# A hybrid conformer and dilated-attention trunk on one core: chunk 6 convolved with banded matrices that are loaded, a first stage in another order, and other rules for what GpSimd may take at a handover

## The chip, the cores and the metric

One core of one Trainium2 chip runs the whole kernel. The metric is device time in microseconds (us) of one execution, as the median of several runs.

## The reference

Two layers over 512 positions of width 1024. Layer 0 is a conformer convolution module and a gated feed-forward block (FFN); layer 1 is dilated attention with three branches and another FFN. Keys and values are projected once, after layer 0.

```python
def conformer_conv_module(h, w_in, b_in, dw, dw_b, ln_g, ln_b, w_out, b_out):
    u = h @ w_in + b_in
    u = u[..., :D_MODEL] * jax.nn.sigmoid(u[..., D_MODEL:])
    u = causal_dwconv(u, dw, dw_b)              # width 31, per channel
    u = layer_norm(u, ln_g, ln_b)               # over the 1024 channels
    u = jax.nn.silu(u)
    return u @ w_out + b_out

for i in range(DEPTH):                          # DEPTH = 2, N_A = 1
    h = rms_norm(x, mix_pre_g[i])
    y = conformer_conv_module(h, ...) if i < N_A else dilated_mixture_attention(h, ...)
    x = x + rms_norm(y, mix_post_g[i])
    x = x + rms_norm(conv_ffn(rms_norm(x, ffn_pre_g[i]), ...), ffn_post_g[i])
```

## The kernel before

Activations lie transposed: channels on the 128 partitions, 512 positions along the free axis, so that the 1024 channels are eight *chunks* (KC = 8). Every matrix product is made with three fp32r matmuls (`mm3`): weight and activation are each split into a high part (ScalarE: `whi`, `hh`, `uh`, `sh`) and a low part that is what the rounding left (VectorE: `wlo`, `hl`, `ul`, `sl`), and high x high, high x low and low x high are added up in PSUM. Weights come as 242 *units* of at most 128x1024 in the order in which TensorE uses them. `loader` issues their DMAs on SyncE's queue (SP) into two `raw` buffers; `splitter` makes the high part on ScalarE and the low part on VectorE or, where a line of its code finds GpSimd (Pool) early enough, on Pool. A ring holds 7 split units.

**The order of all five engines is written out by the builder.** Python generators (`spawn`) stand for side chains; each yields until a modelled clock (`Clock`) says that its engine and its operands are ready, and the instruction is put into the program there. `Clock.cost` holds the durations of that model; TensorE's were columns / 2400 + 0.0015 us for one pass. What is emitted is a fixed order per engine: a wrong guess of the model is a wait on the chip.

**The conformer stage** has these parts.
- *First loop* (`conformer`, L1060 on): for each of 8 input chunks the splits `hh` and `hl` and the square of x, which Pool makes for chunks 0 to 4 (`SQ_POOL`) and ScalarE for the others; VectorE adds the squares into `xacc` inside the same loop. TensorE takes the first two units as the splits come. `rchain` turns `xacc` into the scale `R` that every eviction of the stage needs.
- *Gate*: per chunk m two products (`cig`, `cia`) of 24 matmuls each; `gate` evicts them with R, a sigmoid and a product to `u`.
- *Depthwise convolution of 31 taps*, in three ways. Chunks in `CONV_PE` (1, 3, 5) go to TensorE as fp32 matmuls (`cv`) with banded matrices `T`, nine tiles per chunk that Pool builds out of a small table (`conv_taps`), 36 matmuls per chunk; their u goes through DRAM to another layout (`ud`, `ug`) and the result comes back the same way (`od`, `co`). Chunks 0, 2 and 4 are done tap by tap on VectorE, the last `POOL_TAPS` of them on ScalarE and Pool. Chunks in `MIXES` (6, 7) are split by halves of 256 positions: the first `MIX_PE` taps (17 and 20) on TensorE as three fp32r matmuls each with diagonal matrices (`cm`), the others on VectorE. Their input product is made by halves as well (`cim`). `MIX_PLAN` orders them: a and b are the input products of the first and second half, c and d the tap matmuls.
- *Layer norm*: `stat_acc` gathers sums of the chunks on Pool as they come and marks "stats"; `layer_norm` for each half adds the last chunk of `MIXES`, makes scale and shift and applies them (`ln`, `sh`, `sl`); `conv_out` is the product `wo`.

**A handover** is the change from one block's output to the next block's input: after the conformer (to the first FFN), after the first FFN (to keys and values, `kq`), after attention (to the second FFN). There `Junction.chain` (once for each half `hf`) makes two RMS norms out of sums on TensorE (`st`), a power on Pool (`rst`) and a broadcast (`bc`), and VectorE and ScalarE update x and split it. In `splitter`, `quiet` keeps the low splits of units near a handover off Pool: those from `QUIET[0]` before to `QUIET[1]` after the first unit of the next block; `chains` > 0 does the same, and is raised only inside `stat`.

Of the kernel before, what the change touches and what calls it, by code (L numbers as in the profile page):

```python
# [21 lines left out]
KC = 8  # L22
# [8 lines left out]
N_STAGED = 2  # L31
CONV_PE = (1, 3, 5)
MIXES = (6, 7)
MIX_PE = (17, 20)
MAIN_BANKS = 7
TURN = 8
SLACK = 0.3
POOL_BIAS = -1
QUIET = (3, 5)
SPILL_GAP = 2.5  # L40
# [6 lines left out]
P_CDVE = 3.5  # L47
POOL_TAPS = (8, 8, 4)
P_PTAPS = 3.5
# [135 lines left out]
class Clock:  # L185
# [28 lines left out]
    def cost(self, kind, name, out, ins):  # L214
        n = 1
        for d in out.shape[1:]:
            n *= d
        if name in ("tensor_reduce", "matmul", "transpose"):
            m = 1
            for d in ins[-1 if name == "matmul" else 0].shape[1:]:  # L220
                m *= d
            n = m
        if kind == "dve":
            fast = name in ("tensor_copy", "tensor_scalar") and len(ins) == 1 and ins[0].space == bass.MemoryType.SB
            scal = 0.065 if len(ins) > (2 if name == "scalar_tensor_tensor" else 1) and name[-6:] != "tensor" else 0.0
            scal = 0.065 if name == "scalar_tensor_tensor" and len(ins) > 2 else scal
            return 0.067 + scal + n / (1920.0 if fast else 960.0)
        if kind == "act":
            return (0.075 if name == "copy" else 0.188 if len(ins) > 1 else 0.094) + n / 1200.0
        if kind == "pool":  # L230
            if n <= 8:
                return 0.3 + 0.165 * n
            return 0.15 + n / 476.0
        passes = 4 if ins[0].dtype == F32 else 1
        if name == "transpose":
            return 0.107
        if passes == 1:
            return max(n, 256) / 2400.0 + 0.0015
        return 4 * max(n, 128) / 2400.0 + 0.0015

# [55 lines left out]
class Junction:  # L296
# [59 lines left out]
    def chain(self, hf, rest=None):  # L356
# [92 lines left out]
class Builder:  # L449
    def __init__(self, tc, ctx, x_d, w_d, vec_d, cvec_d, const_d, out_d):  # L450
# [4 lines left out]
        self.vec_d, self.const_d = vec_d, const_d  # L455
        nc = self.nc
# [206 lines left out]
    def splitter(self):  # L663

        nc, free = self.nc, self.clock.free
        for u in range(2, len(self.order)):
# [10 lines left out]
            at = self.clock.ready(hi[:, :w])  # L677
            if u not in self.quiet and not self.chains and max(free["pool"], at) + w / 476.0 + POOL_BIAS < max(free["dve"], at) + w / 960.0:
# [126 lines left out]
    def conv_taps(self, w_idx, Ts):  # L805

        nc = self.nc
        cv = self.c2("cv", F32, (128, 148))
        nc.sync.dma_start(cv, self.cvec_d[w_idx])
        T = []  # L810
        for q in range(ND):
            yield self.when("pool", cv)
            t = self.c2("T", F32, (128, 4, 32, 4))
            wv = cv[:, q * 16:q * 16 + 16].rearrange("p (d f) -> p d f", d=4)
            nc.gpsimd.tensor_tensor(t, self.chan[:, None, :, None].to_broadcast([128, 4, 32, 4]),
                                    wv[:, :, None, :].to_broadcast([128, 4, 32, 4]), op=ALU.mult)
            T.append(t)
        Ts[w_idx] = (T, cv)
        self.mark(("T", w_idx))

    def conv_pe(self, u_of, CO):
# [23 lines left out]
        def back(i, m, pc, cv):  # L845
            og = self.c2("og", F32, (128, 4, 128))
            yield self.when("act", pc)
            for g in range(4):
                nc.scalar.activation(og[:, g], pc[:, g * 128:(g + 1) * 128], AF.Identity,
                                     bias=cv[:, 144 + g:145 + g])  # L850
            self.done(pc)
# [9 lines left out]
        for i, m in enumerate(CONV_PE):  # L861
# [5 lines left out]
            for g in range(4):  # L867
                for d in range(ND):
                    nc.tensor.matmul(pc[:, g * 128 + d:(g + 1) * 128],
                                     T[(g * ND + d) // 4][:, (g * ND + d) % 4].rearrange("p c f -> p (c f)"),  # L870
                                     ug[:, g, :128 - d], start=d == 0, stop=d == ND - 1)
                    if d % 3 == 2:
                        yield W_CONV
# [185 lines left out]
    def conformer(self):  # L1059
# [5 lines left out]
        acc = self.c2("xacc")  # L1065
        sq = []

        def add(c):
            nc.vector.tensor_tensor(acc, sq[0] if c == 1 else acc, sq[c], op=ALU.add)

        for k in range(KC):
            g = self.v("mix_pre0", k)
            self.split_hi(Hc[k], full, self.X[k], g)
            self.split_lo(Hc[k], full, self.X[k], g)
            if k < len(PIECES):
                self.first_units(k)
            t = self.c2("sq")
            if k < SQ_POOL:
                nc.gpsimd.tensor_tensor(t, self.X[k], self.X[k], op=ALU.mult)
            else:  # L1080
                nc.scalar.activation(t, self.X[k], AF.Square)
            sq.append(t)
            if k > ADD_LAG:
                add(k - ADD_LAG)
        for c in range(KC - ADD_LAG, KC):
            add(c)
        self.next_unit = 2
# [723 lines left out]

def pack_cvec(inp):
    dw, dwb = inp["cm_dw"][0], inp["cm_dw_b"][0]
    out = np.zeros((len(CONV_PE), 32, 4, 148), np.float32)
    for i, m in enumerate(CONV_PE):
        for g in range(4):
            c = m * 128 + g * 32 + np.arange(32)
            for f in range(4):
                for d in range(ND):
                    for fo in range(4):  # L1820
                        s = 4 * d + fo - f
                        if 0 <= s <= 30:
                            out[i, :, f, g * 36 + d * 4 + fo] = dw[30 - s, c]
                out[i, :, f, 144 + g] = dwb[c]
    return out.reshape(len(CONV_PE), 128, 148)

# [23 lines left out]
```

## Time and profile before

| | |
|---|---|
| median of 3 runs | 1517.67 us (1514.81 to 1517.68) |
| the profiled execution | 1521.31 us, its span 1519.5 us |
| TensorE busy (matmul) | 1487.6 us, 98% |
| VectorE, ScalarE, GpSimd busy | 951.3, 603.8, 284.3 us |
| mean granted TensorE clock | 0.987 |

Matmuls are pipelined and their ends are modelled, so TensorE counts as busy in nearly all stretches; what a stage loses is seen only when the count of its matmuls, times the distance from start to start of two of them, is set against its length. The conformer stage lies at 0 to 224 us of the span, the first FFN from 224, keys, queries, values and attention from 597 to 1076, the output product and the second FFN after that.

### The profile page before, as it was taken

The page shows a single profiled execution, that of the slowest core. Times are in us where ns is not written, and L with a number is a line of the kernel's source. Part 1 is how long each engine was busy: PE and PEld are TensorE (multiplying, and loading weights), DVE is VectorE, ACT ScalarE, POOL GpSimd, SP SyncE. Part 2 cuts the span into 40 slices and gives each one's busy share as a digit, 9 for nine tenths or more (in the row PEclk, how much of TensorE's full clock was granted, in tenths as well). Part 3 has the DMA queues.
Part 4 walks back from the last instruction along what each step waited for, and adds up shares of the span by engine and source line. Part 5 has one row for each costly group of instructions (what it writes and reads, how often), then busy time and mean ns, then how long its engine had stood idle before and what let it go on. Part 6 is the DMA issues. An engine that isn't in the chain of part 4 may idle for free.

```text
span 1519.5 us, 19622 instructions
## 1 busy us (share of the span) xinstructions
PE 1487.6 (98%) x7778; PEld 1282.5 (84%) x7778; DVE 951.3 (63%) x1428; ACT 603.8 (40%) x1020; POOL 284.3 (19%) x169
## 2 busy tenths in 40 slices
PE   8999999999999999899999999999999999999997
PEld 6889998888888889789888889888898888888887
DVE  6997858946754758822556621566568846754745
ACT  5475465443432426423323222322355444432423
POOL 5894102301210200100000000100002301210212
PEclk9999999999999999999999999999999999999999
DMA  5430322333232222432222223222222332332311
GB/s 178 152 116 29 98 70 84 101 122 97 91 101 85 97 70 70 136 128 84 82 71 69 71 97 97 69 70 84 97 70 84 111 118 91 97 97 90 102 45 56
DMA packets 46891, 139.77 MB, mean 92 GB/s; under 512 B 5072, under 2 KB 10960, under 8 KB 46800
## 3 DMA queue, kind: packets, MB, share of 16 engines
q1 hardware_dynamic: 42768, 135.38, 27.9%
q10 hardware_dynamic: 4032, 3.15, 0.7%
q8 instruction: 61, 1.00, 0.3%
q14 instruction: 30, 0.25, 0.1%
HBM read 132.74 MB, written 5.77 MB: 91 GB/s over the span
## 4 chain that ended last, share of the span: by engine, by line
PE 86%; DVE 3%; ACT 1%; issue 1%; POOL 1%; DMA 0%; POOLq 0%; DVEq 0%; ACTq 0%
PE fi L171 31%; PE kq L171 17%; PE fo L171 16%; PE v L171 9%; PE wo L171 6%; PE sc L171 2%; PE pw L171 1%; PE cm L171 1%; PE pt L171 1%; PE pv L171 1%; PE cim L171 1%; DVE xacc L171 0%; DVE hl L171 0%; DVE mc L171 0%; PE st L171 0%
## 5 line engine op out<-in xcount | busy, mean ns | idle before, releaser
L171 ACT CAST whi<-raw 128x1024 fp32r<-128x1024 f32 (+2 forms) x242 | 248.3, 1027 | 545.7 <-PE fi L171 162.3
L171 POOL TENSOR_TENSOR wlo<-raw,whi 128x1024 fp32r<-128x1024 f32 (+1 forms) x71 | 172.1, 2425 | 929.3 <-ACT whi L171 929.1
L171 DVE TENSOR_TENSOR wlo<-raw,whi 128x1024 fp32r<-128x1024 f32 (+2 forms) x171 | 211.8, 1239 | 167.6 <-ACT whi L171 166.7
L171 PE MATMUL fi<-hl,whi 128*128 128x512 f32 (+1 forms) x768 | 289.3, 377 | 1.1 <-DVE hl L171 1.1
L171 PE MATMUL fi<-hh,whi 128*128 128x512 f32 (+1 forms) x768 | 290.2, 378 | 0.0
L171 PE MATMUL fi<-hh,wlo 128*128 128x512 f32 (+1 forms) x768 | 289.1, 376 | 0.0
L171 PEld LDWEIGHTS fi<-hl,whi 128*128 128x128 f32 x768 | 145.2, 189 | 29.2 <-DVE hl L171 1.3
L171 PEld LDWEIGHTS fi<-hh,whi 128*128 128x128 f32 x768 | 145.3, 189 | 28.2
L171 PEld LDWEIGHTS fi<-hh,wlo 128*128 128x128 f32 x768 | 145.2, 189 | 28.1
L171 PE MATMUL kq<-hh,whi 128*128 128x512 f32 (+1 forms) x416 | 165.0, 397 | 0.0
L171 PE MATMUL kq<-hl,whi 128*128 128x512 f32 (+1 forms) x416 | 157.6, 379 | 5.0 <-DVE hl L171 5.0
L171 PE MATMUL kq<-hh,wlo 128*128 128x512 f32 (+1 forms) x416 | 157.7, 379 | 0.7 <-DVE wlo L171 0.7
L171 PE MATMUL fo<-uh,whi 128*128 128x512 f32 (+1 forms) x416 | 150.1, 361 | 0.0
L171 PE MATMUL fo<-uh,wlo 128*128 128x512 f32 (+1 forms) x416 | 149.8, 360 | 0.0
L171 PE MATMUL fo<-ul,whi 128*128 128x512 f32 (+1 forms) x416 | 149.7, 360 | 0.0
L171 DVE SCALAR_TENSOR_TENSOR cc<-z,vec,cc 128x511 f32<-128x511 f32 (+1 forms) x176 | 142.6, 832 | 8.2 <-ACT cc L171 5.5
L171 DVE TENSOR_TENSOR z<-fi,R 128x512 f32<-128x512 f32 x88 | 60.1, 689 | 92.9 <-PE fi L171 89.2
L171 PEld LDWEIGHTS kq<-hl,whi 128*128 128x128 f32 x416 | 79.2, 190 | 17.3 <-DVE hl L171 5.4
L171 PEld LDWEIGHTS kq<-hh,wlo 128*128 128x128 f32 x416 | 78.7, 189 | 16.5 <-DVE wlo L171 0.9
L171 DVE TENSOR_TENSOR kq<-kq,R 128x512 f32<-128x512 f32 x48 | 46.0, 966 | 71.2 <-PE kq L171 70.5
L171 PEld LDWEIGHTS fo<-uh,whi 128*128 128x128 f32 x416 | 78.4, 188 | 12.8
L171 PEld LDWEIGHTS kq<-hh,whi 128*128 128x128 f32 x416 | 79.1, 190 | 11.9
(210 smaller groups left out, 2594.1 us busy)
## 6 DMA issues: line engine op xcount, KB each, us to landing
raw<-in_w_dram SPq DMA_DIRECT2D x222, 512.0 KB, 3.5
raw<-in_w_dram SPq DMA_DIRECT2D x18, 384.0 KB, 3.1
x<-in_x_dram SPq DMA_DIRECT2D x16, 256.0 KB, 4.3
xs<-x SPq DMA_DIRECT2D x8, 256.0 KB, 4.5
x<-xs SPq DMA_DIRECT2D x8, 256.0 KB, 5.7
out_dram<-x SPq DMA_DIRECT2D x16, 128.0 KB, 1.8
ud<-u ACTq DMA_DIRECT2D x3, 256.0 KB, 2.0
ug<-ud ACTq DMA_DIRECT2D x3, 256.0 KB, 2.7
```

The lines of the kernel that those rows point to most:

```text
L171: return f(*a, **k)
```

## The change

It does seven things. (1) Chunk 6 moves from `MIXES` to `CONV_PE`; chunk 7 alone is mixed, with 15 taps on TensorE in place of 20, and its order is a7 b7 c7 d7. (2) The matrices T are packed on the host and loaded: nine DMAs of 256 KB per chunk on SP's queue, two chunks ahead (`T_AHEAD`). (3) Chunk 4 gives 8 taps to ScalarE and Pool in place of 4. (4) In the first stage all squares are made on ScalarE and added on VectorE by side chains of low rank (`P_SQ`) after the splits. (5) The low splits of units under 6 stay on VectorE (`POOL_FROM`). (6) `QUIET` ends 1 unit after a handover's start in place of 5, but `chains` is raised from the first `chain` of a junction (not the last junction) to its end. (7) The model's TensorE durations are other ones.

```diff
-CONV_PE = (1, 3, 5)
-MIXES = (6, 7)
-MIX_PE = (17, 20)
+CONV_PE = (1, 3, 5, 6)
+MIXES = (7,)
+MIX_PE = (15,)
-QUIET = (3, 5)
+QUIET = (3, 1)
-POOL_TAPS = (8, 8, 4)
+POOL_TAPS = (8, 8, 8)
-SQ_POOL = 5
-ADD_LAG = 2
+P_SQ = 3
+POOL_FROM = 6
-MIX_PLAN = 'a6 a7 c6 c7 b6 b7 d6 d7'
+MIX_PLAN = 'a7 b7 c7 d7'
-T_AHEAD = 3
+T_AHEAD = 2
@@ Clock.cost
-        passes = 4 if ins[0].dtype == F32 else 1
         if name == "transpose":
-            return 0.107
-        if passes == 1:
-            return max(n, 256) / 2400.0 + 0.0015
-        return 4 * max(n, 128) / 2400.0 + 0.0015
+            return 0.111
+        if ins[0].dtype == F32:
+            return 4 * max(n, 128) / 2300.0
+        return max(n, 256) / 2286.0 + 0.0065
@@ Junction.chain
+        if hf == 0 and not self.last:
+            b.chains += 1
...
         b.mark((self, hf, "R"))
+        if hf == 1 and not self.kv:
+            b.chains -= 1
...
             yield from b.stat(self.rm, self.xacc, [slice(q, 512, 4) for q in range(4)])
+            b.chains -= 1
@@ splitter
-            if u not in self.quiet and not self.chains and ...
+            if u >= POOL_FROM and u not in self.quiet and not self.chains and ...
@@ conv_taps
-        cv = self.c2("cv", F32, (128, 148))
-        nc.sync.dma_start(cv, self.cvec_d[w_idx])
+        cv = self.small("cvb", [128, 4])
         for q in range(ND):
-            yield self.when("pool", cv)
-            t = self.c2("T", F32, (128, 4, 32, 4))
-            wv = cv[:, q * 16:q * 16 + 16].rearrange("p (d f) -> p d f", d=4)
-            nc.gpsimd.tensor_tensor(t, self.chan[...], wv[...], op=ALU.mult)
+            yield self.when("sp")
+            t = self.c2("T", F32, (128, 4, 128))
+            nc.sync.dma_start(t.rearrange("p d c -> p (d c)"), self.band_d[w_idx, :, q * 512:(q + 1) * 512])
             T.append(t)
+        nc.sync.dma_start(cv, self.cvec_d[w_idx])
@@ conformer
-            t = self.c2("sq")
-            if k < SQ_POOL:
-                nc.gpsimd.tensor_tensor(t, self.X[k], self.X[k], op=ALU.mult)
-            else:
+        def squares():
+            for k in range(KC):
+                yield self.when("act", self.X[k])
+                if k == 0:
+                    nc.scalar.activation(acc, self.X[k], AF.Square)
+                    continue
+                t = self.c2("sq")
                 nc.scalar.activation(t, self.X[k], AF.Square)
-            sq.append(t)
-            if k > ADD_LAG:
-                add(k - ADD_LAG)
+                self.spawn(add(k, t), P_SQ)
...
+        self.spawn(squares(), P_SQ)
         self.next_unit = 2
         self.spawn(self.loader(), 0)
...
         def rchain():
+            yield from self.until("xacc0")
```

## Rows read from the trace of the kernel before

**Rows 1.** The page's first part: busy time, share and count of each engine.
```profile
PE 1487.6 (98%) x7778; PEld 1282.5 (84%) x7778; DVE 951.3 (63%) x1428; ACT 603.8 (40%) x1020; POOL 284.3 (19%) x169
```

**Rows 2.** Stretches: length; PE, PEld, DVE, ACT, POOL busy (count); granted clock; DMA share, GB/s.
```profile
5.10:27.30 22.20, 17.79 (x48) 12.24 (x49) 19.16 (x19) 11.22 (x16) 10.47 (x6) 0.85 0.72 256
27.30:102.90 75.60, 73.77 (x398) 62.37 (x397) 70.52 (x90) 40.31 (x69) 67.41 (x49) 1.00 0.40 125
102.90:171.20 68.30, 65.98 (x521) 65.47 (x520) 56.81 (x116) 42.16 (x109) 28.05 (x20) 0.93 0.24 74
171.20:224.00 52.80, 50.76 (x412) 50.35 (x411) 33.02 (x74) 26.67 (x54) 3.99 (x4) 0.97 0.24 71
224.00:251.20 27.20, 26.10 (x216) 25.46 (x215) 22.91 (x54) 12.60 (x30) 6.30 (x4) 1.00 0.14 48
...
587.40:631.10 43.70, 37.39 (x303) 36.67 (x302) 40.93 (x94) 26.54 (x60) 8.76 (x7) 0.97 0.18 55
631.10:1076.60 445.50, 445.50 (x2185) 388.58 (x2186) 214.21 (x355) 135.31 (x242) 21.55 (x9) 1.00 0.28 89
...
1120.00:1160.00 40.00, 38.03 (x308) 37.53 (x308) 33.32 (x76) 21.03 (x50) 6.39 (x5) 0.96 0.23 69
```

**Rows 3.** The chain that ended last: start us, length us, what.
```profile
157.94 13.23 PE cm L171 x111
...
251.08 55.08 PE fi L171 x237
```

**Rows 4.** Timeline of TensorE: start us, length us, engine, operation, tiles, form, count.
```profile
84.36 0.82 PE L171 MATMUL cv<-ug,T 128*128 128x125 f32 x6
...
85.73 0.82 PE L171 MATMUL cv<-ug,T 128*128 128x122 f32 x6
```

**Rows 5.** Timeline of all engines in the first stage; the bracket: idle before, releaser.
```profile
16.66 5.19 POOL L171 TENSOR_TENSOR wlo<-raw,whi 128x1024 fp32r<-128x1024 f32 x2 [2.30 <-ACT whi L171]
16.70 2.92 DVE L171 SCALAR_TENSOR_TENSOR hl<-x,vec,hh 128x512 fp32r<-128x512 f32 x1
...
19.54 2.87 DVE L171 TENSOR_TENSOR xacc<-xacc,sq 128x512 f32<-128x512 f32 x1
...
23.12 0.50 PE L171 MATMUL cig<-hl,whi 128*128 128x512 f32 x1 [1.80 <-DVE hl L171]
...
23.59 0.74 DVE L171 SCALAR_TENSOR_TENSOR hl<-x,vec,hh 128x512 fp32r<-128x512 f32 x1
```

**Rows 6.** Waits of TensorE: who waited for whom, us in total, times, longest.
```profile
PE kq L171 <- DVE hl L171: 5.0, 1, 5.0
...
PE cv L171 <- DVE ca L171: 1.8, 1, 1.8
...
PE st L171 <- POOL m L171: 1.6, 1, 1.6
```

**Rows 7.** Timelines of ScalarE's queue, TensorE and Pool: chunk 5's way through the convolution.
```profile
108.53 0.34 ACTq L171 DMA_DIRECT2D ud<-u  x1
...
118.26 0.83 PE L171 MATMUL cv<-ug,T 128*128 128x128 f32 x6
...
133.17 0.38 ACTq L171 DMA_DIRECT2D od<-og  x1
...
142.76 1.48 POOL L171 TENSOR_TENSOR s<-s,sq 128x512 f32<-128x512 f32 x1
```

**Rows 8.** The chain that ended last, around the second half's layer norm.
```profile
180.27 0.79 PE lst L171 x8
...
187.25 27.55 PE wo L171 x215
```

**Rows 9.** Timelines of Pool and VectorE in the second handover.
```profile
616.20 2.47 POOL L171 TENSOR_TENSOR wlo<-raw,whi 128x1024 fp32r<-128x1024 f32 x1 [8.07 <-ACT whi L171]
616.34 2.61 DVE L171 SCALAR_TENSOR_TENSOR hl<-x,vec,hh 128x256 fp32r<-128x256 f32 x1
```

**Rows 10.** Stretches of 5 us (columns as in rows 2).
```profile
5.00:10.00 5.00, 4.50 (x9) 2.75 (x10) 2.97 (x5) 2.58 (x5) 1.14 (x2) 1.00 0.96 355
```

More of the change, by code (lines that the diff above doesn't have):

```diff
@@ L449, with __init__ @@
 class Builder:
-    def __init__(self, tc, ctx, x_d, w_d, vec_d, cvec_d, const_d, out_d):
+    def __init__(self, tc, ctx, x_d, w_d, vec_d, cvec_d, band_d, const_d, out_d):
         self.now = 0.0
@@ L454, in __init__ @@
         self.x_d, self.w_d, self.cvec_d, self.out_d = x_d, w_d, cvec_d, out_d
-        self.vec_d, self.const_d = vec_d, const_d
+        self.vec_d, self.band_d, self.const_d = vec_d, band_d, const_d
         nc = self.nc
@@ L677, in splitter @@
             at = self.clock.ready(hi[:, :w])
-            if u not in self.quiet and not self.chains and max(free["pool"], at) + w / 476.0 + POOL_BIAS < max(free["dve"], at) + w / 960.0:
+            if u >= POOL_FROM and u not in self.quiet and not self.chains and max(free["pool"], at) + w / 476.0 + POOL_BIAS < max(free["dve"], at) + w / 960.0:
                 eng = nc.gpsimd
@@ L807, in conv_taps @@
         nc = self.nc
-        cv = self.c2("cv", F32, (128, 148))
-        nc.sync.dma_start(cv, self.cvec_d[w_idx])
+        cv = self.small("cvb", [128, 4])
         T = []
         for q in range(ND):
-            yield self.when("pool", cv)
-            t = self.c2("T", F32, (128, 4, 32, 4))
-            wv = cv[:, q * 16:q * 16 + 16].rearrange("p (d f) -> p d f", d=4)
-            nc.gpsimd.tensor_tensor(t, self.chan[:, None, :, None].to_broadcast([128, 4, 32, 4]),
-                                    wv[:, :, None, :].to_broadcast([128, 4, 32, 4]), op=ALU.mult)
+            yield self.when("sp")
+            t = self.c2("T", F32, (128, 4, 128))
+            nc.sync.dma_start(t.rearrange("p d c -> p (d c)"), self.band_d[w_idx, :, q * 512:(q + 1) * 512])
             T.append(t)
+        nc.sync.dma_start(cv, self.cvec_d[w_idx])
         Ts[w_idx] = (T, cv)
@@ L849, in back @@
                 nc.scalar.activation(og[:, g], pc[:, g * 128:(g + 1) * 128], AF.Identity,
-                                     bias=cv[:, 144 + g:145 + g])
+                                     bias=cv[:, g:g + 1])
             self.done(pc)
@@ L869, in conv_pe @@
                     nc.tensor.matmul(pc[:, g * 128 + d:(g + 1) * 128],
-                                     T[(g * ND + d) // 4][:, (g * ND + d) % 4].rearrange("p c f -> p (c f)"),
+                                     T[(g * ND + d) // 4][:, (g * ND + d) % 4],
                                      ug[:, g, :128 - d], start=d == 0, stop=d == ND - 1)
@@ L1065, in conformer @@
         acc = self.c2("xacc")
-        sq = []
-        def add(c):
-            nc.vector.tensor_tensor(acc, sq[0] if c == 1 else acc, sq[c], op=ALU.add)
         for k in range(KC):
@@ L1076, in conformer, with add @@
                 self.first_units(k)
-            t = self.c2("sq")
-            if k < SQ_POOL:
-                nc.gpsimd.tensor_tensor(t, self.X[k], self.X[k], op=ALU.mult)
-            else:
-                nc.scalar.activation(t, self.X[k], AF.Square)
-            sq.append(t)
-            if k > ADD_LAG:
-                add(k - ADD_LAG)
-        for c in range(KC - ADD_LAG, KC):
-            add(c)
+        def squares():
[5 more added lines that the diff above has]
+                t = self.c2("sq")
+                nc.scalar.activation(t, self.X[k], AF.Square)
+                self.spawn(add(k, t), P_SQ)
+        def add(k, t):
+            while added[0] < k - 1:
+                yield 0.05
+            yield self.when("dve", t, acc)
+            nc.vector.tensor_tensor(acc, acc, t, op=ALU.add)
+            added[0] += 1
+            if added[0] == KC - 1:
+                self.mark("xacc0")
+        added = [0]
+        self.spawn(squares(), P_SQ)
         self.next_unit = 2
@@ L1809, in pack_vec, with pack_band @@
     return np.ascontiguousarray(np.concatenate([src[n].reshape(-1, 128).T for n, _ in VECS], 1))
[L1812 to L1815, printed above, removed]
+def pack_band(inp):
+    dw = inp["cm_dw"][0]
+    out = np.zeros((len(CONV_PE), 32, 4, 4, ND, 32, 4), np.float32)
+    i = np.arange(32)
+    for j, m in enumerate(CONV_PE):
         for g in range(4):
-            c = m * 128 + g * 32 + np.arange(32)
             for f in range(4):
@@ L1822, in pack_cvec @@
                         if 0 <= s <= 30:
-                            out[i, :, f, g * 36 + d * 4 + fo] = dw[30 - s, c]
-                out[i, :, f, 144 + g] = dwb[c]
-    return out.reshape(len(CONV_PE), 128, 148)
+                            out[j, i, f, g, d, i, fo] = dw[30 - s, m * 128 + g * 32 + i]
+    return out.reshape(len(CONV_PE), 128, 4 * ND * 128)
+def pack_cvec(inp):
+    dwb = inp["cm_dw_b"][0]
+    out = np.zeros((len(CONV_PE), 32, 4, 4), np.float32)
+    for j, m in enumerate(CONV_PE):
+        for g in range(4):
+            out[j, :, :, g] = dwb[m * 128 + g * 32:m * 128 + g * 32 + 32, None]
+    return out.reshape(len(CONV_PE), 128, 4)
 def kernel(**inputs):
@@ L1834 @@
         "cvec": pack_cvec(inp),
+        "band": pack_band(inp),
         "const": host_consts(),
```

## The prediction

> **What bounds the kernel now.** I read the page's engine shares first: TensorE is busy for 98% of the span [rows 1], so only its own work and the places where it stands or runs slowly can move the end. The busy share hides those places, because the ends of matmuls are modelled. So I took the distance from start to start: 237 matmuls of 512 columns in 55.08 us are 0.232 us each, and 111 of 256 columns in 13.23 us are 0.119 us each [rows 3]. Then I cut the span into stages and set count times distance against each length [rows 2]. The reader is to see that the stretch from 631 to 1077 us is busy without a break, while the time is lost in few places. The first two units need 48 x 0.232 = 11.2 us and take 22.2: 11.0 lost, of which 0.15 x 22.2 = 3.3 to the granted clock of 0.85 (part of the time at 1.2 GHz in place of 2.4). From 102.9 to 171.2 us stand 192 `cim` and 222 `cm` at 0.119 and one chunk of `cv` (8.1, below): 57.4 of 68.3, so 10.9 go to short sums, waits and a clock of 0.93. The `wo` stretch has 384 x 0.119 = 45.8 of 52.8. The three handovers hold 216, 303 and 308 matmuls at 0.119, which is 25.7 of 27.2, 36.1 of 43.7 and 36.7 of 40.0: 1.5, 7.6 and 3.3 lost. Last I read who ended TensorE's waits [rows 6].
>
> **Chunk 6 and the taps of chunk 7: TensorE's own work.** Chunk 6 loses 17 taps x 2 halves x 3 = 102 matmuls of 0.119, chunk 7 loses 5 x 2 x 3 = 30: -15.7 us. Added are 36 fp32 matmuls. Two groups of three `cv` start 1.37 us apart with three 512-column matmuls between [rows 4], so a group costs 1.37 - 0.70 = 0.67 us and a chunk 12 x 0.67 = 8.1. Chunk 6's input product changes from 96 x 0.119 = 11.4 to 48 x 0.232 = 11.2. Sum: **-7.9 us**, all on the path, the surest term (-7 to -8.5).
>
> **First stage.** VectorE's last `hl` starts at 23.59, and TensorE waits for one at 23.12 [rows 5]. Before it in VectorE's queue stand four additions into `xacc`, one held to 2.87 us, and an `hl` held to 2.92 where the clean one takes 0.74; both lie beside squares or low splits on Pool [rows 5]. Without them the last `hl` leaves 2.9 + 2.2 + 3 x 0.7 = 7.2 us earlier. TensorE then becomes the limit: 36 matmuls of chunks 2 to 7 are 8.4 us at the full clock. The start, until the first weights are there, stays. I take **-6 us** of the 11.0 lost; if half-clock stretches remain as long as now, -3; at most -8. The squares go to ScalarE behind the splits, their seven additions behind the `hl`, the low splits of units 2 to 5 to VectorE. All this is covered by TensorE's first two products and delays only R, which no one needs before the third pair of PSUM banks is full, some 33 us (three products of 11.2) after the start. Without that cover each added microsecond would count once.
>
> **The middle.** One `cv` group waits 1.8 us for a bank that VectorE's tap chain holds, one `st` 1.6 us for Pool's sums [rows 6]. 27 builds of T leave Pool, which is busy for 67 of 75.6 us [rows 2], and VectorE loses chunk 6's 13 taps x 2 and four taps of chunk 4. I take **-1.8** (0 to -4).
>
> **The loads of T.** 36 DMAs of 256 KB are 9.4 MB. The weights' stretch moves 125 GB/s over 75.6 us [rows 2], and the same queue has reached 355 GB/s [rows 10]. With T it would be 250 GB/s. SP's queue is passed by nothing else than weight loads; each waits there for a free `raw` buffer. The cover is the ring: six units ahead at 24 x 0.232 = 5.6 us are 33 us. Cost 0; what it costs uncovered is the third rival. T's own buffers fall from 27 to 18 in flight.
>
> **Layer norm, the step that I trust least.** Before, the first half's norm ran behind the second half's products. After, it needs chunk 6, which is the last to come and makes two trips through DRAM. Chunk 5's trip gives the legs [rows 7]: its product ends at 102.9 [rows 2], `cv` begins 15.4 us later, `og` leaves 14.9 us after that, Pool's last sum ends 11.1 us after `og`. From the last sums on TensorE to the first `wo` are 7.0 us [rows 8]. Let E6 be the end of chunk 6's product. Chunk 5's `cv` begins 15.4 - 11.2 = 4.2 us after E6 and takes about 12.5 when mixed with other matmuls, so chunk 6's begins at E6 + 16.7; with 14.9 + 11.1 + 7.0 the product `wo` can start at E6 + 49.7. TensorE's work after E6 is 11.4 for a7 and b7, 16.2 for two chunks of `cv`, 90 x 0.119 = 10.7 for c7 and d7 and about 1.5 of short sums: 39.8. So it stands some **10 us** in a place where it did not, and I add what the clock costs behind such a stop, 0.03 x 52.8 = 1.6 us in the `wo` stretch with its one stop [rows 2]: `wo` at E6 + 51.3 (45 if each leg is as short as it can be without Pool's holds, 58 if each adds 1 to 3 us). Against that, the second half's stop goes, because c7 and d7 are done by then: the `wo` stretch becomes about 49 in place of 52.8. E6 itself is 102.9 - 6 - 1.8 + 11.2 = 106.3. The stage ends at 106.3 + 51.3 + 49 = 206.6, not 224.0: **-17.4 us** in all, so the norm and its surroundings bring -1.7 beside the three terms above (-9 to +7).
>
> **Handovers.** Pool's low split from 616.20 holds an `hl` of VectorE to 2.61 us, until Pool has ended [rows 9]; the same happens four times in the three handovers (once, twice, once), and the long wait of `kq` for `hl`, 5.0 us [rows 6], lies behind two of them. After, the chain's whole length is closed to Pool. VectorE gets the four splits itself, about 1.3 us each (an estimate: twice the columns of the 0.74 row less its fixed part), in place of a hold of 2.1: net -0.9 x 4, and of the half-clock time behind the stops, 0.03 x 43.7 + 0.04 x 40 = 2.9 us, about half: **-5 us**. What VectorE does more is covered only where TensorE has staged matmuls; if TensorE waits for each added split instead, it is +5. Low end -9. After the chain, units 1 to 4 behind the start may now go to Pool, which the old `QUIET` forbade: that is in the +3 that I keep as the upper end.
>
> **TensorE's durations in the model.** The old model has 512 columns at 0.215 us, the trace 0.232. Short matmuls (`sc`, `pt`, `st`, `bc`) are therefore placed 8% late in the program, and no wait is seen from 631 to 1077 us. With the right figure they stand just where the model has their operands ready, and a Pool hold of 2 us can reach them. Pool has 9 instructions in that stretch [rows 2]: nothing or, at the worst, 9 x 2.1 = 19 us. The value lies nearest to the row that shows no wait: **+1**, and 4 as far as the range goes. Elsewhere the better order may gain as much.
>
> **Sum.** -17.4 - 5 + 1 = -21.4 us on 1521.3 us of the profiled execution (span 1519.5 and 1.8 around it), so 1499.9. That execution lies 3.6 us above the median of the runs, 1517.7; I shift by that: **1496.3 us**.
>
> **Rivals.** *The late chunk is later.* Every leg of chunk 6's trip grows and `wo` starts at E6 + 58 to 62, because its gate queues behind VectorE's taps: +7 to +11, some 1505. For it: chunk 5's gate needed 5.6 us before `ud` left. Against: 26 tap instructions less on VectorE. Chance 0.15. *The handovers do not get quieter*: VectorE, busy for 40.9 of 43.7 us in the second [rows 2], becomes the bound with added splits: +5 for -5, and with waits in attention +4, some 1508. Chance 0.13. *The loads of T stand before the weights*, the one that ends slower: if a T load waits on SP's queue for its buffer, the weights behind it wait too, and once more than the ring's 33 us are used up TensorE stops. At most all of T goes by while it stands: 9.4 MB at 355 GB/s are 26.6 us, so 1496 + 27 = 1523. Against: 18 buffers in place of 27, and two thirds of the bandwidth free [rows 2]. Chance 0.06. The Trainium skill, "DMA: Bandwidth & Descriptors", section "Queues, rings and completion order", says that each DMA engine takes one queue's descriptors in ring order, which is what would make this so; no run here shows T and weights on one queue yet. *The change does not do what it says* (T late, Pool still inside the chains): only TensorE's work falls, 1510. Chance 0.05.
>
> **How the numbers follow.** The forecast has the remaining 0.61. The terms' good ends together (-8.5, -8, -4, -9, -9, 0) would give 1479, which I hold for unlikely at once; half of that distance is 1487. Upwards the first two rivals and the last belong inside, so 1511. About 0.2% (3 us) is what a measurement of this kernel can tell from no change: faster than 1514.6 holds the forecast, the first two rivals and most of the last, 0.89; within, 0.05; slower than 1520.7, the loads' rival, 0.06.
>
> **What would show it.** Right: the first two units end near 21.5 us of the span; 90 `cm` in place of 222; `wo` starts near 158 us and ends near 207, after a stop of about 10 us; no `wlo` on Pool between the first `rst` and the last of a handover, and no VectorE row above 2 us there; the stretch of attention still without waits. Wrong: a wait of TensorE or ScalarE for `raw` between 30 and 100 us (the loads), or waits for `T`; a stop before `wo` of 20 us or more; `sc`, `pt` or `px` in the list of TensorE's waits.

## The result, and the profile after

The changed kernel takes **1497.5 us** (median of four runs, 1497.0 to 1498.1), against 1516.8 (1514.8 to 1517.7) for the kernel before beside it: a ratio of 0.9875, 95% interval 0.9858 to 0.9892. The forecast was 1496.3 us, in a range of 1487 to 1511. The time is right to 0.1%, but by luck: the gain comes from a cause that no step named, and the edits that the steps priced at -21 us are together worth about nothing, although some of the terms hold. What follows shows both.

The profiled execution took 1498.06 us, its span 1496.3. First line of its page, as in [rows 1]:

```profile
PE 1454.2 (97%) x7670; PEld 1265.6 (85%) x7670; DVE 907.8 (61%) x1431; ACT 593.8 (40%) x983; POOL 159.3 (11%) x106
```

TensorE's busy time fell by 33.4 us for 108 records fewer, although 72 of the new ones belong to 36 long fp32 matmuls, which leave two records each. 7.9 of that was expected. So I took the distance from start to start once more, in a stretch that the change does not touch, the first feed-forward. The chain that ended last, after, between 260 and 480 us (start us, length us, what):

```profile
336.35 87.04 PE fi L171 x384
423.39 43.52 PE fo L171 x192
```

and the same view of the kernel before:

```profile
339.61 89.24 PE fi L171 x384
```

The same 384 matmuls of 512 columns take 0.2267 us each and not 0.2324, as [rows 3] also has it. Both kernels run this stretch without a break at the full granted clock. A kernel has some 4,800 matmuls of this width: at 5 to 6 ns each that is 24 to 29 us, more than the whole gain. Matmuls of 256 columns come at medians of 0.118 to 0.122 us before and 0.120 after. ScalarE's rows are as before; VectorE's differ where Pool holds fewer of them (below).

Stretches of after, the first four cut at the same events as in [rows 2], the last one in the second handover (length; PE, PEld, DVE, ACT, POOL busy with counts; granted clock; DMA share, GB/s):

```profile
5.10:20.10 15.00, 12.75 (x48) 9.26 (x49) 12.41 (x18) 12.54 (x20) 0.00 (x0) 1.00 0.82 291
20.10:125.50 105.40, 91.35 (x469) 77.82 (x468) 83.83 (x110) 54.38 (x98) 51.80 (x35) 0.92 0.60 203
125.50:172.00 46.50, 43.97 (x348) 43.19 (x348) 32.20 (x67) 12.77 (x27) 12.54 (x9) 0.92 0.34 111
172.00:221.70 49.70, 48.31 (x405) 48.10 (x404) 32.30 (x80) 33.14 (x68) 1.50 (x2) 1.00 0.18 54
...
588.50:622.00 33.50, 28.01 (x222) 27.38 (x221) 31.60 (x73) 20.89 (x45) 3.71 (x4) 0.93 0.30 97
```

The first stage is 7.2 us shorter. The second row holds one chunk of products more (48 x 0.227 = 10.9 us) but is 29.8 us longer, and its clock fell from 1.00 to 0.92. The conformer ends at 221.7 us instead of 224.0; the forecast had 206.6. The second handover is still the place where VectorE is busy nearly all the time (31.6 of 33.5 us). Who ended TensorE's waits, after (us in total, times, longest), beside [rows 6]:

```profile
PE cv L171 <- DMA ug<-ud: 7.8, 2, 7.6
PE cv L171 <- issue: 6.0, 1, 6.0
PE kq L171 <- DVE hl L171: 4.4, 1, 4.4
PE py L171 <- DVE fr L171: 2.9, 2, 1.5
```

The first two rows are not in [rows 6] under these names, and both lie in the stretch where T is loaded. The third is the old wait of the second handover, hardly shorter. The fourth is new, in attention.

**The first new stop.** Timeline of after, TensorE and the DMA queues of SP and ScalarE (start us, length us, engine, line, operation, tiles, count; in brackets the idle time before and its releaser):

```profile
66.97 9.09 SPq L171 DMA_DIRECT2D T<-in_band_dram  x8
67.56 0.38 ACTq L171 DMA_DIRECT2D ug<-ud  x1
75.38 0.98 PE L171 MATMUL cv<-ug,T 128*128 128x128 f32 x3 [7.58 <-DMA ug<-ud]
```

and stretches of 5 us around it (columns as above):

```profile
65.00:70.00 5.00, 2.80 (x19) 2.20 (x17) 4.96 (x8) 4.16 (x10) 2.67 (x3) 1.00 0.65 203
70.00:75.00 5.00, 0.00 (x0) 0.00 (x0) 5.00 (x8) 0.70 (x1) 3.36 (x3) 0.62 1.01 322
75.00:80.00 5.00, 4.62 (x17) 4.27 (x18) 5.00 (x9) 2.11 (x3) 0.99 (x1) 0.50 0.82 256
```

Of the nine loads of T of this chunk six go out within 3.5 us on SP's queue (the other three from 75.3 on), and the shuffled chunk `ug`, 256 KB that TensorE needs at that moment, starts 0.6 us behind the first of them on ScalarE's queue. It lands after 7.7 us; in the kernel before the same transfer of the same chunk took 4.2. The DMA engines are full (1.01), and the clock is at half (1.2 GHz) for the 5 us behind TensorE's idle time. How long the transfers took between 5 and 130 us (KB each, median us from issue to landing), after:

```profile
T<-in_band_dram SPq DMA_DIRECT2D x36, 256.0 KB, 5.9
ug<-ud ACTq DMA_DIRECT2D x3, 256.0 KB, 3.5
od<-og ACTq DMA_DIRECT2D x2, 256.0 KB, 7.4
```

and before:

```profile
ug<-ud ACTq DMA_DIRECT2D x3, 256.0 KB, 2.7
od<-og ACTq DMA_DIRECT2D x2, 256.0 KB, 3.2
```

**The second new stop** has the same root at one remove. ScalarE's timeline of after:

```profile
95.32 0.40 ACTq L171 DMA_DIRECT2D od<-og  x1
...
103.29 0.37 ACTq L171 DMA_DIRECT2D co<-od  x1
103.75 0.59 ACT L171 COPY nm<-bc 128x512 f32<-128x512 f32 x1 [4.91 <-DMA od<-og]
...
116.75 0.34 ACTq L171 DMA_DIRECT2D ud<-u  x1
```

The way back of the second loaded chunk meets the next group of T loads and takes 8.0 us. ScalarE, which issues the load of `co` in its own queue, stands for 4.9 us; taps, diagonals, weight casts and the gate of the third loaded chunk queue up behind, and `ud` of that chunk leaves at 116.75. TensorE runs out of products at 115.7 and stands 6.0 us ("issue" in the list of waits), until that chunk's `ug` lands at 121.6.

### The profile page after: what moved, and what is told of

The parts are those of the page before. It is cut to its first block, busy times and chain, and to the rows that moved or that the text cites. A ratio compares the mean times of both kernels' runs of the same rounds, so it can differ in the third digit from the quotient of the medians.

```text
span 1496.3 us, 19325 instructions
## 1 busy us (share of the span) xinstructions
PE 1454.2 (97%) x7670; PEld 1265.6 (85%) x7670; DVE 907.8 (61%) x1431; ACT 593.8 (40%) x983; POOL 159.3 (11%) x106
## 4 chain that ended last, share of the span: by engine, by line
PE 89%; DVE 6%; DMA 2%; ACT 1%; issue 1%; POOL 0%; SPq 0%; ACTq 0%; POOLq 0%; DVEq 0%
PE fi L171 32%; PE kq L171 17%; PE fo L171 16%; PE v L171 9%; PE wo L171 6%; PE sc L171 2%; PE cv L171 2%; PE cia L171 1%; DVE mc L171 1%; DMA raw<-in_w_dram 1%; PE pw L171 1%; PE pt L171 1%; PE pv L171 1%; DMA T<-in_band_dram 1%; DVE wlo L171 1%
## 5 line engine op out<-in xcount | busy, mean ns | idle before, releaser
L171 DVE TENSOR_TENSOR wlo<-raw,whi 128x1024 fp32r<-128x1024 f32 (+1 forms) x204 | 251.6, 1234 | 166.8 <-ACT whi L171 166.6
L171 PE MATMUL fi<-hh,whi 128*128 128x512 f32 (+1 forms) x768 | 286.3, 373 | 0.0
L171 PE MATMUL fi<-hh,wlo 128*128 128x512 f32 (+1 forms) x768 | 285.4, 372 | 0.8 <-DVE wlo L171 0.8
L171 PE MATMUL fi<-hl,whi 128*128 128x512 f32 (+1 forms) x768 | 285.3, 371 | 0.0
L171 POOL TENSOR_TENSOR wlo<-raw,whi 128x1024 fp32r<-128x1024 f32 (+1 forms) x38 | 84.8, 2233 | 1010.3 <-ACT whi L171 1007.2
L171 PEld LDWEIGHTS fo<-ul,whi 128*128 128x128 f32 x416 | 78.6, 189 | 11.3
```

The costliest lines, as they stand in the source:

```text
L171: return f(*a, **k)
```

## The experiments

Ratios are to runs of the kernel before on the same chip, with 95% intervals.

**Is it the address?** The change adds four small tiles for the biases. Each takes 32 bytes per partition in the pool of small tiles, so all tiles of the main pool (`hh`, `hl`, `u`, `x`, `y`, T and the others) start 128 bytes later than before, while the weights `whi` and `wlo` stay where they were. This is read from the addresses of the compiled programs: modulo 256 bytes the weights lie at 192 in both kernels, the main pool at 64 before and at 192 after. The kernel before with nothing but this shift:

```diff
+        for _ in range(4):
+            nc.vector.memset(self.small("pad", [128, 4]), 0.0)
```

> The kernel before with one thing added: four unused tiles of 4 columns in the small pool (four memsets), which move every tile of the main pool up by 128 bytes in SBUF, as the changed kernel's new cvb tiles do. Theory A (where the moving operand lies sets the pace): 512-column matmuls come every 227 ns as in the changed kernel, not every 232, and with about 4800 of them the time falls by some 20 to 25 us, to 1492 to 1497. Theory B (the pace of 227 belongs to a chip, a run or the new order): they stay at 232 ns and the time at 1515 to 1518.

And the changed kernel without the shift, its bias tiles put into slots of the main pool:

```diff
-        cv = self.small("cvb", [128, 4])
+        cv = self.c2("cvb", F32, (128, 4))
```

> The changed kernel with its four small cvb tiles put into slots of the main pool, so that the main pool starts at the address that it had before. Theory A: 232 ns and some 20 to 25 us more than the changed kernel, 1516 to 1523, about the time before: the edits proper are worth nothing or cost up to 6 us. Theory B: 227 ns and 1496 to 1499.

The kernel before, shifted, took 1496.1 us, ratio 0.985 (0.9831 to 0.987). The changed kernel, not shifted, took 1519.7, ratio 1.0012 (1.0002 to 1.0021). The chain of the first, and then of the second, in the first feed-forward:

```profile
336.23 87.04 PE fi L171 x384
```

```profile
336.70 89.60 PE fi L171 x384
```

So 128 bytes of shift bring the whole gain, 0.227 in place of 0.232 to 0.233 us, and all the edits of the change together bring +0.1% without it. This is shown from both sides.

**Which address?** Two more kernels: the changed one with 64 bytes more (two more such small tiles), and the kernel before with 128 bytes ahead of everything, so that weights and main pool move together.

```diff
+        for _ in range(2):
+            nc.vector.memset(self.sp.tile([128, 4], F32, tag="pad", ...), 0.0)
```

> The changed kernel with two more unused tiles of 4 columns, so that the main pool starts 64 bytes further, at a multiple of 512 bytes. Theory A, if the pace is set by how operands lie in lines of 128 or 512 bytes: a third pace, 214 to 226 ns, and 1440 to 1496 us. If only one bit of the address counts: 227 or 232 ns, 1497 or 1520. Theory B: 227 ns and 1496 to 1499.

```diff
+        nc.vector.memset(self.cp.tile([128, 32], F32, name="pad"), 0.0)
```

> The kernel before with one unused 128-byte tile in the pool of constants, so that the weights and the main pool both move by 128 bytes and their distance stays. If the address of the moving operand alone sets the pace of the 512-column matmuls, this is the shifted kernel once more: 227 ns from start to start and about 1496 us. If the distance between the moving operand and the weights sets it, the pace stays at 232 ns and the time at about 1517 us. If only the weights' address counts, something else, up to 10 us to either side.

With both moved, the time is 1516.9 us, ratio 0.9982 (0.9973 to 0.9991), and the pace is the old one although the main pool has the "good" address:

```profile
336.08 89.23 PE fi L171 x384
```

So it is the distance between the moving operand and the weights that counts (the `raw` buffers move with the weights). No traffic of other engines is needed for it: in the kernel before, 191 matmuls of 512 columns that stream `hh` or its like run while VectorE, ScalarE and Pool stand still and no transfer is under way, and their median is 232 ns; 182 such ones in the shifted kernel have 227. With 64 bytes the time is 1504.7, ratio 0.991 (0.989 to 0.993):

```profile
334.93 87.89 PE fi L171 x384
```

There the three products of a triple differ: `hh,whi` 226 ns, `hl,whi` 229, `hh,wlo` 232, a mix that no theory had.

**Other distances**, on the changed kernel with spaced loads of T (below): 256, 192 and 32 bytes more ahead of the main pool, by one unused tile in the pool of small tiles.

```diff
+        nc.vector.memset(self.sp.tile([128, 64], F32, tag="pad", ...), 0.0)   # 64, 48 or 8 columns
```

> The changed kernel with spaced loads of T (1488.6 us in the run before) and 256 bytes more ahead of the main pool, which puts it at 192 modulo 512, as the weights are. If what counts is that the main pool and the weights differ modulo 512, some pace between 226 and 238 ns: at 226 ns about 1484 us, at 233 ns about 1516 us. If any shift that is a multiple of 128 bytes is as good as another, 1488 us.

> Spaced loads of T and 192 bytes more ahead of the main pool: its distance to the weights is 192 modulo 256 (0 gave 227 ns, 128 gave 232, 64 gave 226 to 232). If the pace depends on how far the two lie apart, whichever way, this is the kernel with 64 once more: 512 columns at 226 to 232 ns, 256 columns at 113 to 118, about 1495 us. If only a distance of 0 is good, 232 ns and about 1510 us.

> Spaced loads of T and 32 bytes more ahead of the main pool: distance 32 modulo 256. If the pace goes gradually with the distance, some 227 to 229 ns and 1489 to 1497 us; if it steps at a granule of 64 bytes or more, 227 ns and 1488 us.

They took 1489.4, 1510.5 and 1512.1 us; ratios 0.9805 (0.9779 to 0.9831), 0.9948 (0.9929 to 0.9967) and 0.996 (0.9946 to 0.9974). 256 bytes change nothing: as far as this one step tells, what counts is the distance modulo 256. With 192, and then with 32, the chains of the first feed-forward and of the `wo` stretch (256 columns):

```profile
169.91 15.09 PE wo L172 x133
...
325.95 89.60 PE fi L172 x384
```

```profile
170.31 31.50 PE wo L172 x270
...
328.60 89.60 PE fi L172 x384
```

The wide matmuls go at 0.233 us in both, but the narrow ones at 0.1135 and 0.1167, faster than the 0.120 of the changed kernel. So at 192 the wide matmuls and the time came out as the second theory has it (only 0 is good), the narrow ones as the first (192 like 64). For comparison, the narrow ones of the changed kernel:

```profile
179.46 32.39 PE wo L171 x270
```

All distances that ran, with the start-to-start medians of the products that stream `hh`, `hl`, `uh`, `ul` (256 columns: `sh` and `sl` as well):

| distance modulo 256 | kernels | 512 columns, ns | 256 columns, ns |
|---|---|---|---|
| 0 | after; before shifted by 128; spaced T; the same shifted by 256 | 226 to 227 | 120 |
| 32 | spaced T, shifted by 32 | 234 | 116 to 117 |
| 64 | after, shifted by 64 | 226, 229, 232 | 113 to 118 |
| 128 | before; after unshifted; before, both shifted | 231 to 234 | 118 to 122 |
| 192 | spaced T, shifted by 192 | 233 to 234 | 113 to 114 |

In the products `v`, where the weights stream and `hh` or `hl` is loaded, it is 231 to 232 ns at 0, 239 to 240 at 128, 233 at 192, 235 to 236 at 32 and 236 to 238 at 64.

My theory for 32 bytes (gradual, or a granule of 64 bytes and more) fell: 32 bytes cost as much as 128. That the matmul's reads of the moving operand and the loading of the next weights meet in the memory would fit the dependence on a distance, but it is argued only; the runs don't show where they meet.

**The loads of T.** The changed kernel with 2 us of the model's time between the loads:

```diff
+            yield T_GAP        # 2.0, after each load of T
```

> The changed kernel with the loads of T spread: 2 us of the model's time between two of them in place of back to back. Theory: the two new stops of TensorE before cv (7.7 and 6.1 us, with slow clock behind) come from T loads that share the DMA engines with the ud, ug, od and co transfers of the chunks; spread, those transfers take 2 to 4 us again, both stops shrink to under 2 us, and the time is 8 to 14 us below the changed kernel's 1497.5. Rival: the stops come from late gates on VectorE and ScalarE; then spreading moves the time by less than 3 us.

1488.6 us, ratio 0.9802 (0.9781 to 0.9823), 9 us less than the change. The stops of 7.6 and 6.0 us are down to 1.4 ("issue" in the list) and 3.3 us (`dl` there); both still end 0.1 us behind the landing of a `ug` (73.69 and 113.20). Another stop, `st` for Pool's `m`, has come up. The transfers did not all fall to 2 to 4 us, as I had expected: on the chip up to four loads of T still go out within 1.5 us, and between 5 and 130 us the median of `od` fell from 7.4 to 2.7 us, but that of `ug` rose from 3.5 to 4.7 and that of `co` from 4.0 to 5.9. The `ug` of the first stop takes 5.3 us (7.7). So of the 6.2 us by which that stop shrank the shorter transfer is 2.3; the other 3.9 are products that TensorE now has left behind the issue of `ug`. The second stop shrank because `od` of the second chunk is back after 2.7 us (8.0), so that `ud` of the third chunk leaves at 105.1 in place of 116.75. Waits of TensorE up to the end of the conformer:

```profile
PE cv L172 <- ACT dl L172: 3.3, 1, 3.3
PE st L172 <- POOL m L172: 2.8, 1, 2.8
...
PE cv L172 <- issue: 1.4, 1, 1.4
```

**Chunk 6 undone**, loads of T spaced as well:

```diff
-CONV_PE = (1, 3, 5, 6)
-MIXES = (7,)
-MIX_PE = (15,)
+CONV_PE = (1, 3, 5)
+MIXES = (6, 7)
+MIX_PE = (17, 20)
-MIX_PLAN = 'a7 b7 c7 d7'
+MIX_PLAN = 'a6 a7 c6 c7 b6 b7 d6 d7'
-POOL_TAPS = (8, 8, 8)
+POOL_TAPS = (8, 8, 4)
```

> The changed kernel with spaced loads of T, but chunk 6 stays on VectorE's and TensorE's taps as before (three loaded chunks, the old plan of the two mixed chunks). By my steps chunk 6's move takes about 4 us from TensorE (102 matmuls of 0.119 less 8.1), while the layer norm takes a stop of 10 us and gives back 3.8: then this kernel is about as fast or up to 4 us slower, 1488 to 1493, with the first wo at 167 to 171 us. If the late chunk costs more than its work saves, it is faster: 1482 to 1486.

1491.3 us, ratio 0.9817 (0.9799 to 0.9835): not to be told apart from the 0.9802 with chunk 6 moved. `wo` starts earlier than I expected, at 160.7 us, and the conformer ends at 211.6 (212.8 with chunk 6 moved). Its longest wait of TensorE there; the `dl` and "issue" rows of the kernel with spaced loads are not in its list:

```profile
PE st L172 <- POOL m L172: 3.0, 1, 3.0
```

**The handovers and the model's durations**, each undone on the kernel with spaced loads:

```diff
-QUIET = (3, 1)
+QUIET = (3, 5)
-            b.chains += 1      # and both decrements
```

> The changed kernel with spaced loads of T, and the handovers as before: Pool may take the low splits of units 1 to 4 of the chain's far end again and the units behind the start are closed to it. By my step, quiet handovers are worth 5 us (up to 9): then this gives 1493.6 (to 1497.6), and the second handover loses 2 to 4 us more. By the rival (VectorE becomes the bound with added splits) quiet handovers cost what they save or more: 1483.6 to 1488.6.

```diff
-            return 0.111
+            return 0.107
-            return 4 * max(n, 128) / 2300.0
-        return max(n, 256) / 2286.0 + 0.0065
+            return 4 * max(n, 128) / 2400.0 + 0.0015
+        return max(n, 256) / 2400.0 + 0.0015
```

> The changed kernel with spaced loads of T and the model's old TensorE durations (512 columns at 0.215 us, 256 at 0.108). By my step, new durations cost +1 (0 to +4) through waits of short matmuls in attention: then this gives 1487.6 (1484.6 to 1488.6), and the two waits of py for fr (2.9 us each, 1.6 us lost each) go. If the measured durations help elsewhere (a better order around the loads and the layer norm), this is slower: 1491 to 1496.

They took 1490.5 and 1489.5 us, ratios 0.981 (0.9795 to 0.9825) and 0.9799 (0.9781 to 0.9817): in the whole, neither is to be told apart from 0.9802. In the parts they do something, and it cancels. Loud handovers against quiet ones, by stretches of the two profiled executions: the first feed-forward with its handover 368.7 against 366.9 us, the second with its own 369.8 against 367.6, but the second handover and attention 473.9 against 477.0. The first and the third handover are better quiet (by 1.9 and 2.3 us), the second is worse (by 3.1). TensorE's waits in the kernel with loud handovers around the first and the third, and in attention:

```profile
PE st L172 <- DVE xacc L172: 2.2, 2, 1.4
...
PE py L172 <- DVE fr L172: 3.0, 2, 1.5
...
PE st L172 <- DVE xacc L172: 1.4, 1, 1.4
```

The `st` waits are not there with quiet handovers; in return the wait of `kq` for `hl` is not there with loud ones. With the old durations (and quiet handovers) the first feed-forward takes 364.5 us (366.9) and the second handover with attention 475.2 (477.0), but the conformer ends at 215.9 (212.8). The waits of `py` for `fr` are gone, but `kq` waits longer:

```profile
PE kq L172 <- DVE hl L172: 7.5, 1, 7.5
```

**Put together**: spaced loads of T, the first and third handovers quiet and the second as before, old durations from the end of the conformer on.

```diff
-        if hf == 0 and not self.last:
+        if hf == 0 and not self.last and not self.kv:
             b.chains += 1
...
-            b.chains -= 1      # the one of the second handover
...
-        starts = [self.index["fi", 0, NF], self.index["k", 0, 0], self.index["fi", 1, NF]]
-        return {u for s in starts for u in range(s - QUIET[0], s + QUIET[1])}
+        starts = [(self.index["fi", 0, NF], 1), (self.index["k", 0, 0], 5), (self.index["fi", 1, NF], 1)]
+        return {u for s, n in starts for u in range(s - QUIET[0], s + n)}
...
+        if self.free["pe"] > T_OLD:        # 212.0
+            if name == "transpose":
+                return 0.107
+            return (4 * max(n, 128) if ins[0].dtype == F32 else max(n, 256)) / 2400.0 + 0.0015
```

> The changed kernel with spaced loads of T, with quiet handovers 1 and 3 but the second one as before, and with the old TensorE durations from 212 us of the model on. By the stretches of the runs before: the loud second handover gains 3.1 us between the first kq and the first wo of attention, the old durations gain 2.4 in the first feed-forward and 1.9 in attention: 1488.6 - 7.4 = 1481. If the two gains in attention are one and the same waits, 1483. If neither is more than the scatter of an order, 1488.

1485.6 us, ratio 0.9778 (0.9759 to 0.9797), the fastest that ran; its interval still overlaps that of spaced loads alone. The second handover and attention take 473.2 us (477.0 with spaced loads alone): the waits of `py` are gone, and that of `kq` is the old one. The first feed-forward takes 366.7, so the 2.4 us that the old durations seemed to bring there did not come again.

```profile
PE kq L173 <- DVE hl L173: 5.0, 1, 5.0
```

The wait of `kq` in the second handover over both switches, from the lists of waits of these kernels:

| | new durations | old durations |
|---|---|---|
| quiet | 4.4 us (after; spaced T) | 7.5 us |
| as before | none, but 2.4 for `st` | 5.0 us (before; the last kernel) |

Here the measured durations help (3 us and more) and the quiet rule harms, while in attention the measured durations bring the two waits of `py`.

## Why the time was right and the reasons were not

I cut the spans at the same events (first matmul of each stage) and set against each length the count of matmuls times the kernel's own median distance; what is left is lost time. The kernel before, shifted, has the pace of the changed one, so these two columns differ by the edits alone. Length / lost, us:

| stretch | before, shifted | after | T spaced | T spaced, chunk 6 undone |
|---|---|---|---|---|
| first two units | 21.1 / 10.2 | 15.0 / 4.1 | 14.8 / 3.9 | 15.0 / 4.1 |
| to the first `wo` | 143.3 / 11.1 | 151.9 / 26.8 | 143.5 / 18.4 | 140.6 / 8.4 |
| `wo` | 53.0 / 4.4 | 49.7 / 2.0 | 49.6 / 1.9 | 50.9 / 2.3 |
| first feed-forward | 365.7 / 1.4 | 366.8 / 2.5 | 366.9 / 2.5 | 367.8 / 3.4 |
| second handover, attention | 472.6 / 12.3 | 476.9 / 16.7 | 477.0 / 16.7 | 476.4 / 16.0 |
| second `wo` | 55.2 / 1.1 | 54.6 / 0.5 | 54.6 / 0.5 | 54.6 / 0.5 |
| second feed-forward | 371.0 / 5.2 | 367.6 / 1.8 | 367.6 / 1.8 | 367.7 / 1.9 |

After less the shifted kernel: -6.1 + 8.6 - 3.3 + 1.1 + 4.3 - 0.6 - 3.4 = +0.6 us. The forecast had -21.4 for the same edits. The shift alone brought 21.7 (1517.8 less 1496.1); that the two sizes agree is luck.

- **TensorE's work, -7.9: right.** Length less lost of the first three rows is 191.7 us before and 183.7 after, -8.0.
- **First stage, -6: right, and for the reason given.** It ended at 20.1 us (forecast: near 21.5), 7.2 us earlier than [rows 2] has it and 6.1 at equal pace. Pool does nothing in it, six `hl` run without a hold in 4.05 us, and the granted clock went from 0.85 to 1.00. VectorE's row:

```profile
11.26 4.05 DVE L171 SCALAR_TENSOR_TENSOR hl<-x,vec,hh 128x512 fp32r<-128x512 f32 x6
```

- **The middle, -1.8: one wait was misread, the other came back.** The `cv` of 1.8 us in [rows 6] did not wait for a bank that VectorE's taps hold: in the kernel before `ug` leaves at 78.55 and lands at 82.78, and `cv` starts at 82.92, as close behind it as in after (75.24 and 75.38). Of the two things that it waits for in the compiled program, VectorE's, a `co`, was done at 67.1 us. In the shifted kernel the list names the transfer itself:

```profile
PE cv L171 <- DMA ug<-ud: 1.4, 1, 1.4
```

  So TensorE already stood for `ug` before, and the loads of T made this wait longer and did not remove it. The wait of `st` for Pool's `m` left the list of after, but with spaced loads, with and without chunk 6 moved, it is back with 2.8 and 3.0 us (1.6 in [rows 6]).
- **The loads of T, 0: this step failed.** It cost two stops, 13.6 us together, and what the clock lost behind them; up to the first `wo` 15.7 us more are lost than in the shifted kernel. Spaced loads bring 8.4 of them back in this stretch, 9 in the whole time; the rest stays in the shorter stops for `ug` and in a wait of `st`. I had compared mean rates (250 GB/s needed, 355 reached) and named the ring of weights as the cover. The weights were covered: TensorE's list up to the first feed-forward has 0.4 us for `whi`, as before, and ScalarE's waits for `raw` between 28 and 172 us are 8.6 us in all, 11.5 before; the rival that put T ahead of the weights did not come true. (A wait of ScalarE for `raw`, which I had named as the sign of it, was a poor sign, since the kernel before has it as well.) But the step looked at one queue only. The shuffles of the convolution go over ScalarE's queue to the same DMA engines, have no buffer ahead, and TensorE or ScalarE waits for some of them. The Trainium skill, "DMA: Bandwidth & Descriptors", section "Issuing engines are not separate DMA queues", says that transfers issued by different engines run on the same 16 DMA engines and interleave. The trace agrees: 4.2 us became 7.7 for the `ug` of the same chunk beside six loads of T, at a DMA share of 1.01. The mean over 75 us hid that T comes in bursts, six or seven loads in some 3 us.
- **Layer norm, -1.7 net with a new stop of 10 us: the net was about right, the stop was not.** From the end of chunk 6's product (125.5, where `cim` begins) to `wo` (172.0) are 46.5 us, not 51.3. The trip through DRAM was shorter than chunk 5's in [rows 7]: `ud` leaves at 128.55, 3.0 us after the product (5.6 there), `og` at 149.61, 24.1 after it (I had 31.6). From there to `wo` are 22.4 us (I had 18.1). ScalarE's queue, after:

```profile
128.55 0.33 ACTq L171 DMA_DIRECT2D ud<-u  x1
...
149.61 0.37 ACTq L171 DMA_DIRECT2D od<-og  x1
```

  No stop of 10 us appears, only two waits of `lst` for Pool's sums, 1.6 and 0.8 us, and a clock of 0.92. The `wo` stretch has 49.7, as forecast (49). Lost from the end of the loaded products to the first feed-forward: 12.9 us in the shifted kernel, 8.7 after. That does not make the move of chunk 6 and its plan a gain: with T spaced it saves 7.9 us of TensorE's work, and 9.6 us more are lost (18.4 against 8.4 before `wo`, 1.9 against 2.3 in it), about half of it before chunk 6's product ends and half behind. Net nothing, as the two times say.
- **Handovers, -5: wrong in size, and one of three in sign.** VectorE's row of 2.6 us beside Pool's low split [rows 9] is gone, and no `wlo` is on Pool in a chain, as said. The third handover gained 3.4 us. The second did not: the chain that ended last, after, shows VectorE as the bound, which was the second rival, in this one place:

```profile
616.58 0.16 DVE var L171
616.75 0.33 DVE kq L171
...
617.26 2.41 DVE kq L171 x3
619.67 0.74 DVE wlo L171
...
620.72 0.89 DVE hl L171 x2
...
621.65 2.36 PE kq L171 x4
```

  Four evictions of `kq` and a low split that Pool may no longer take stand ahead of the `hl` that TensorE waits for, while Pool had been idle for 12.5 us:

```profile
612.32 0.87 POOL L171 TENSOR_TENSOR rst<-var,mhalf 128x2 f32<-128x2 f32 x1 [12.50 <-DVE var L171]
```

- **The model's durations, +1 (0 to +4): right in kind, about 3 us in size.** Two new waits of `py` for `fr`, each 1.5 us; they are there in all nine kernels that ran with the new durations in attention and in none of the five with the old ones. They come the way the step says: a low split on Pool now meets VectorE's chain behind which `py` stands. Two of the eight `nM` are held to 2.0 and 2.3 us (0.16 otherwise), and none with the old durations. After, Pool and VectorE:

```profile
948.20 2.40 POOL L171 TENSOR_TENSOR wlo<-raw,whi 128x1024 fp32r<-128x1024 f32 x1 [5.68 <-ACT whi L171]
948.29 2.32 DVE L171 TENSOR_TENSOR nM<-st,mx 128x4 f32<-128x4 f32 x1
```

  Elsewhere the same figures take work from Pool: behind 250 us it makes 31 to 35 low splits in the kernels with the new durations and 61 to 64 in those with the old ones, and the median of VectorE's `ul` is 0.68 us in place of 2.12. In the feed-forwards, where TensorE is the limit, that brought no time. What they bring in the second handover I had only as "a better order elsewhere".
- **What was missing: the pace.** Every product "count times distance" took 0.232 and 0.119 us from the trace of before as constants of the chip. They are properties of one placement in memory. The forecast's own list of what would show it wrong had no line for a stretch that the change does not touch; such a line would have found this at once. With the +0.6 us that the edits cost in place of -21.4, the forecast would have been about 1518 us, and the unshifted kernel measured 1519.7.

## What to carry to other kernels

Before a gain of one or two per cent is put down to an edit, compare the distance from start to start in a stretch that the edit does not touch; four small tiles were worth more here than a new order of a whole stage, and one run of the old kernel with the same shift tells. Bulk loads are priced by the transfers that they meet, on all queues, and by their bursts, not by the mean rate: ask which short transfer has someone waiting behind it. A rule such as "Pool stays out of the chain" is to be looked at handover by handover, because it saves holds in one and takes away the only idle engine in another.

## What the hardware showed that I had not expected

The pace of back-to-back fp32r matmuls depends on where the moving operand lies relative to the weights: 226 to 227 ns for 512 columns when the two start at a distance that is a multiple of 256 bytes in a partition, 231 to 234 at distances of 32, 128 and 192, mixed at 64. For 256 columns the order is another one: 113 to 114 ns at 192, 113 to 118 at 64, 116 to 117 at 32, 120 at 0, 118 to 122 at 128. Over this kernel that is 1496 against 1517 us. No placement that ran is the best for both widths, and why it is so stays open.
